# First operations of a unit tied behind traced evacuations, VectorE triangles and spread weight fetches in a hybrid attention layer

## The chip, the cores and the metric

The kernel runs on one core of a Trainium2 chip. The metric is device time in microseconds (us) of one execution, the median over the runs shown; lower is better. TensorE is called PE in the views (PEld its weight loads), VectorE is DVE, ScalarE is ACT, GpSimd is POOL and SyncE, which issues most transfers, is SP.

## The reference

One post-norm residual layer over 1024 tokens of width 1024. The mixing width is split into eight forgetting-attention heads (FoX: softmax with a decay from a forget gate) and eight stick-breaking heads, each 64 wide, all with a SiLU gate and one output projection.

```python
def reference(x, c, w_ada, b_ada, w_in, b_f, w_out, ln_g, ln_b):
    ...
    u = (_layer_norm(x) * (1.0 + scale[:, None, :]) + shift[:, None, :]).astype(dtype)
    fq, fk, fv, fg, ff, sq, sk, sv, sg = _split_columns(u @ w_in[layer])
    f_cum = jnp.cumsum(jax.nn.log_sigmoid(ff + b_f[layer]), axis=1).transpose(0, 2, 1)
    ...
        # FoX, per query block
        s = einsum(q, k) * scale + (f_q[..., :, None] - f_k[..., None, :])
        y = einsum(softmax(where(causal, s, -inf)), v)
        # stick-breaking, per query block
        z = einsum(q, k) * scale
        log_keep = where(strict, log_sigmoid(-z), 0.0)
        later = cumsum(log_keep, axis=3, reverse=True) - log_keep
        y = einsum(where(strict, exp(log_sigmoid(z) + later), 0.0), v)
    ...
    y = concatenate([y_fox * silu(fg), y_sb * silu(sg)], axis=-1) @ w_out[layer]
    resid = ALPHA * x + gate[:, None, :] * y
    x = _layer_norm(resid, ln_g[layer], ln_b[layer]).astype(dtype)
```

## The kernel before

**Units.** The sixteen heads are eight pairs p, 0 to 3 stick-breaking and 4 to 7 FoX. A unit (p, h, i) is one block of 128 query rows of one head h of a pair. There are sixteen units to a pair, so 128, and unit 112, called `LAST` in the code, opens pair 7. That pair takes its units by two query blocks, from the longest rows down: (h 0; i 7, 6), (h 1; 7, 6), (h 0; 5, 4) and so on.

**A unit's path.** `att_scores` (L487) issues the score matmuls `S` (L501, L502) into one of two PSUM buffers. For FoX a row operation on VectorE (L508) adds the decay and the mask, which lie in `fb`, to `S`, and writes `a` and the row's extreme `nm`; ScalarE takes the exponential (L514); two small VectorE operations invert the row sum `l` (L515, L516). Then ScalarE and VectorE split the result into two fp16 halves (L480, L481, called a half below; `f` is their room), and SP issues a transposing transfer (L485) into `pt`. For stick-breaking ScalarE takes two sigmoids (L527, L528), VectorE one or two scans (L533, L537), GpSimd a product (L541), and the halves follow (L477, L478). Four units after its scores, `att_pv` issues the `pv` matmuls (L585); ScalarE and VectorE evacuate them to `ty` (L611, L612), GpSimd multiplies by the gate (L614), SP stores.

**Projections beside it.** Between the units TensorE runs projections of the next pair as fillers, each a group of `m` matmuls (L284 to L286) or `v` matmuls (L355 to L357) into one of two accumulators. They are evacuated by a ScalarE and a VectorE operation: q (L255, L256), k (L264, L268 or L272, which write the low part `kl`), the gate (L277, L278, `sg`), v (L366, L367), and the small ones around the scale of v (`bss_sb`, L391 to L397) and the forget rows (`fcum`, L426 to L436).

**Triangles.** `att_causal` (L460) adds the causal triangle to a 128x128 block of `fb` (L465) ahead of each unit's row operation; it is issued behind the row operation of the unit before.

**Output projection.** `load_wo` (L924) fetches a 128-row slab `wor` of the output weights on SP's queue (L936, 512 KB), casts it in two pieces on ScalarE (`woh`, L939) and takes the rest on GpSimd (`wol`, L940). Two slabs are fetched at the first unit of pair 7; the others follow inside `gen_last_g`, the last projection (the gate of pair 7), two steps ahead. `load_ln` fetches the last layer norm's vectors (`lngb`). `o_half` runs the residual of half a block of rows: `gate` times the PSUM accumulator `o` into `r` (L1010), `ALPHA` times `xr` plus `r` (L1011), statistics (L1012). The accumulators `o` and `m` are the same two PSUM buffers.

**Rooms.** Six tiles of tag `att` hold `a`, `f`, `fb`, `kp`, `be` and `r`. Three wider tiles of tag `v` hold the v operands, the raw data of the first four slabs `wor` (two to a tile), `lngb`, the first two blocks' `xr` (`xr_two`), and, in some FoX pairs, two blocks' halves (`room_ff`).

**What sets the order.** TensorE's order is written out by hand by the loop at the end (`FILL`, `G7`, `TAIL` share the fillers out to units). The order on VectorE, ScalarE, GpSimd and SP is made by a scheduler at build time, from the program's dependences. `after(...)` adds an edge for that order only: on the chip each engine runs its own list in order and waits by semaphores for data and rooms alone.

## Time and profile before

| | |
|---|---|
| Median of 3 runs | 666.49 us |
| Lowest, highest | 664.18, 672.92 us |
| The profiled execution | 668.8 us |
| Its span | 667.0 us |
| Mean granted TensorE clock of its span | 0.979 |

The span is the time from the first to the last recorded instruction; the rest of the execution's time, 1.8 us, lies around it. The rows that the prediction rests on are shown there. A row of the timeline has its start, its duration, the engine, the line, the operation with its output and inputs, and, in brackets, how long the engine had been idle before it and what released it. Rows of consecutive equal operations are merged (x6). Tile names are without numbers there; in the order lists below a name has the head, the block and a running number, as `a_0_7_6048` for `a` of head 0, block 7.

### The profile page before, as it was taken

How to read it: one execution, taken by the hardware profiler on the slowest of the kernel's cores; microseconds unless marked ns; L12 is line 12 of the kernel's file. 1: busy time of each engine (PE TensorE's matmuls, PEld its weight loads, DVE VectorE, ACT ScalarE, POOL GpSimd, SP SyncE). 2: the span in 40 equal slices, each digit the busy share in tenths (PEclk: the TensorE clock that was granted, in tenths of full speed). 3: DMA queues.
4: the chain of work that ended last, by engine and by line, in shares of the span. 5: the costliest groups of instructions: out<-in, count | busy, mean ns of one | idle time of the engine just before them, and what ended most of it. 6: DMA issues, size and time to landing. Idle time of an engine off the chain costs nothing.

```text
span 667.0 us, 10848 instructions
## 1 busy us (share of the span) xinstructions
PE 620.2 (93%) x3523; PEld 524.4 (79%) x3523; DVE 494.1 (74%) x878; ACT 403.3 (60%) x803; POOL 413.4 (62%) x529
## 2 busy tenths in 40 slices
PE   5999999999999799998989999999999957799995
PEld 3779898888897678888978888899887736588885
DVE  6785458886869788897678777766888566896856
ACT  5567457876658667776666675766778775430000
POOL 6469978565649675877387454525643599656411
PEclk9999999999999899998999999999999977899998
DMA  9966331114635656556556766755566999552411
GB/s 332 410 254 250 95 96 40 30 29 113 127 75 104 150 90 148 122 134 144 106 145 149 170 145 139 177 134 131 143 139 150 248 240 226 141 156 102 154 64 63
DMA packets 169576, 97.79 MB, mean 147 GB/s; under 512 B 136944, under 2 KB 150576, under 8 KB 169520
## 3 DMA queue, kind: packets, MB, share of 16 engines
q1 hardware_dynamic: 158960, 76.61, 45.6%
q10 hardware_dynamic: 10560, 20.50, 11.3%
q8 instruction: 28, 0.46, 0.3%
q14 instruction: 28, 0.23, 0.1%
HBM read 51.95 MB, written 7.90 MB: 90 GB/s over the span
## 4 chain that ended last, share of the span: by engine, by line
PE 67%; DVE 8%; DMA 7%; issue 6%; ACT 5%; POOL 5%; SPq 1%; ACTq 0%; POOLq 0%; DVEq 0%
PE m L284 8%; PE m L285 7%; PE m L286 7%; PE pv L585 6%; PE o L991 4%; PE o L993 4%; PE o L992 4%; PE S L501 4%; PE S L502 4%; PE v L355 3%; PE v L357 3%; PE v L356 3%; POOL be L541 2%; DMA raws<-in_w_qkg_dram 2%; DMA pt<-kp 2%
## 5 line engine op out<-in xcount | busy, mean ns | idle before, releaser
L284 PE MATMUL m<-uh,whi 128*128 128x512 f32 x304 | 124.3, 409 | 4.5 <-DVE bss_sb L394 2.3
L286 PE MATMUL m<-uh,wlo 128*128 128x512 f32 x304 | 120.4, 396 | 0.0
L285 PE MATMUL m<-ul,whi 128*128 128x512 f32 x304 | 120.3, 396 | 0.0
L541 POOL TENSOR_TENSOR be<-be,kp 128x127 f32<-128x127 f32 (+3 forms) x64 | 86.4, 1351 | 35.5 <-DVE kp L537 19.0
L481 DVE SCALAR_TENSOR_TENSOR f<-a,l,f 128x1024 f16<-128x1024 f32 (+3 forms) x64 | 70.6, 1109 | 24.0 <-ACT f L480 23.3
L614 POOL TENSOR_TENSOR ty<-ty,sg 64x256 f32<-64x256 f32 x64 | 53.4, 835 | 48.8 <-DVE ty L612 30.3
L501 PE MATMUL S<-k,q 128*128 128x512 f32 (+5 forms) x192 | 67.7, 354 | 11.7 <-DVE nm L508 11.7
L533 DVE TENSOR_TENSOR_SCAN kp<-kp,floor 128x512 f32<-128x512 f32 (+2 forms) x64 | 65.1, 1017 | 15.6 <-ACT kp L527 14.6
L284 PEld LDWEIGHTS m<-uh,whi 128*128 128x128 f32 x304 | 57.6, 190 | 15.1 <-DVE bss_sb L394 2.7
L286 PEld LDWEIGHTS m<-uh,wlo 128*128 128x128 f32 x304 | 57.5, 189 | 13.7
L465 POOL TENSOR_TENSOR fb<-fb,causal 128x128 f32<-128x128 f32 x64 | 37.8, 592 | 49.1 <-DVE nm L508 35.6
L514 ACT ACTIVATE a<-a,nm 128x1024 f32<-128x1024 f32 (+3 forms) x64 | 49.6, 774 | 28.9 <-DVE nm L508 27.8
L585 PE MATMUL pv<-pt,v 128*128 128x256 f16 (+1 forms) x560 | 65.3, 264 | 1.3 <-DVE ty L612 0.7
L502 PE MATMUL S<-kl,qz 128*128 128x512 f32 (+5 forms) x192 | 66.3, 346 | 0.0
L285 PEld LDWEIGHTS m<-ul,whi 128*128 128x128 f32 x304 | 57.6, 189 | 9.3
L585 PEld LDWEIGHTS <-v 128*128 128x128 f16 x560 | 48.2, 98 | 17.8 <-issue 10.1
L480 ACT ACTIVATE f<-a,l 128x1024 f16<-128x1024 f32 (+3 forms) x64 | 49.1, 773 | 20.8 <-DVE l L516 13.6
L478 DVE TENSOR_TENSOR kp<-be,kp 128x128 f16<-128x128 f32 (+7 forms) x48 | 50.0, 1042 | 15.0 <-ACT kp L477 14.6
L355 PE MATMUL v<-whi_v,uh 128*128 128x256 f32 (+1 forms) x192 | 56.1, 292 | 3.6 <-DVE kl L268 2.5
L508 DVE CUSTOM_DVE_ANT_0 a<-S,fb 128x1024 f32<-128x1024 f32 (+3 forms) x64 | 48.2, 753 | 10.7 <-POOL fb L465 4.2
L527 ACT ACTIVATE kp<-S 128x128 f32<-128x128 f32 (+3 forms) x64 | 41.6, 651 | 22.8 <-PE S L502 14.9
L357 PE MATMUL v<-wlo_v,uh 128*128 128x256 f32 (+1 forms) x192 | 54.8, 285 | 0.0
(314 smaller groups left out, 1603.2 us busy)
## 6 DMA issues: line engine op xcount, KB each, us to landing
raw<-in_w_qkg_dram ACTq DMA_DIRECT2D x38, 256.0 KB, 2.7
wss<-in_w_ss_dram SPq DMA_DIRECT2D x16, 512.0 KB, 8.4
wg<-in_w_gate_dram SPq DMA_DIRECT2D x8, 512.0 KB, 4.1
fb<-f_dr ACTq DMA_DIRECT2D x8, 512.0 KB, 4.4
wor<-in_w_out_dram SPq DMA_DIRECT2D x8, 512.0 KB, 6.1
out_dram<-r SPq DMA_DIRECT2D x15, 256.0 KB, 2.0
y_dr<-ty SPq DMA_DIRECT2D x56, 64.0 KB, 2.0
x<-in_x_dram SPq DMA_DIRECT2D x6, 512.0 KB, 5.6
```

The costliest lines, as they stand in the source:

```text
L284: nc.tensor.matmul(acc, hi[:, c], u_hi[kt][:, s], start=(kt == 0), stop=False)
L285: nc.tensor.matmul(acc, hi[:, c], u_lo[kt][:, s], start=False, stop=False)
L286: nc.tensor.matmul(acc, lo[:, c], u_hi[kt][:, s], start=False, stop=(kt == NB - 1))
L355: nc.tensor.matmul(acc[:, :n], u_hi[kt][:, ts_], hi[:, s], start=(kt == 0), stop=False)
L357: nc.tensor.matmul(acc[:, :n], u_hi[kt][:, ts_], lo[:, s], start=False, stop=(kt == NB - 1))
L481: nc.vector.scalar_tensor_tensor(second, a3, l, first, op0=ALU.mult, op1=ALU.subtract)
L501: nc.tensor.matmul(S[:, s, :w], qst[p][h][:, qs], kst[p][h][:, ks], start=True, stop=False)
L502: nc.tensor.matmul(S[:, s, :w], z, klo[p][:, ks], start=False, stop=True)
L533: scan = nc.vector.tensor_tensor_scan(rv, rv, floor[0][:, 512 - n:][:, ::-1], initial=0.0, op0=ALU.mult, op1=ALU.max)
L541: nc.gpsimd.tensor_tensor(be[:, :ke - 1], be[:, :ke - 1], kp[:, 1:ke], op=ALU.mult)
L585: nc.tensor.matmul(acc[:, q0:256], vt[p][:, kb, h * P:h * P + P], st_pt[p, h, j][:, 2 * kb + part, q0:], start=start, stop=stop)
L614: nc.gpsimd.tensor_tensor(yt[r, :], yt[r, :], sgt[p][r, qs], op=ALU.mult)
```

## The change

Four things are changed.

1. `ev_ops` remembers the last evacuation's ScalarE and VectorE operation. The next unit's `att_scores` takes them and puts its own first ScalarE operation (the sigmoid, or the exponential) and its first VectorE operation (the scan, or the row operation) behind them, by edges of order alone.
2. The sixteen triangles of pair 7 run on VectorE instead of GpSimd.
3. The output weights' slabs are fetched at the units 111, 113, 114, 115, 117, 118, 119 and 120 instead of two at 112 and the others with the last projection; `load_ln` goes from unit 117 to 119; the halves of pair 6 that use a `v` tile are now blocks 7 to 4 of head 1 and all of head 0, instead of all of head 1 and blocks 5 to 0 of head 0.
4. In `o_half` the product with `gate` is written back into PSUM, and the second operation reads it there and writes `r`.

```diff
+    ev_ops = {}
     def evac_q(p, ch, acc, qst, heads):
...
-            nc.scalar.activation(qst[h][r, s], acc[r, :], AF.Copy, scale=SCALE)
-            nc.vector.scalar_tensor_tensor(qst[h][o, s], acc[r, :], SCALE, qst[h].bitcast(F32)[r, s],
-                                           op0=ALU.mult, op1=ALU.subtract)
+            ev_ops["act"] = nc.scalar.activation(qst[h][r, s], acc[r, :], AF.Copy, scale=SCALE)
+            ev_ops["dve"] = nc.vector.scalar_tensor_tensor(qst[h][o, s], acc[r, :], SCALE, qst[h].bitcast(F32)[r, s],
+                                                          op0=ALU.mult, op1=ALU.subtract)
...
     def evac_k(p, ch, acc, kst, klo, heads):
...
+        ev_ops.update(act=first, dve=last)
         return first, last
...
-        nc.vector.tensor_scalar(power, total, 1.0e-30, 1.0, op0=ALU.max, op1=ALU.mult)
+        ev_ops["dve"] = nc.vector.tensor_scalar(power, total, 1.0e-30, 1.0, op0=ALU.max, op1=ALU.mult)
...
     def att_causal(u):
...
-            nc.gpsimd.tensor_tensor(f[:, dg], f[:, dg], causal, op=ALU.add)
+            (nc.vector if p == 7 else nc.gpsimd).tensor_tensor(f[:, dg], f[:, dg], causal, op=ALU.add)
...
     def att_scores(u, following):
...
+        behind = [ev_ops.pop(e) for e in list(ev_ops)]
...
-            rows = nc.vector.tensor_tensor_reduce(out=v3(a), in0=S[:, :ns, :w], in1=v3(f),
+            with after(*behind):
+                rows = nc.vector.tensor_tensor_reduce(out=v3(a), in0=S[:, :ns, :w], in1=v3(f),
...
-            nc.scalar.activation(a[:, :ke], a[:, :ke], AF.Exp, scale=-1.0, bias=nm, accum_out=l)
+            with after(*behind):
+                nc.scalar.activation(a[:, :ke], a[:, :ke], AF.Exp, scale=-1.0, bias=nm, accum_out=l)
...
-            if p == 4 or (p == 5 and h == 0) or (p == 6 and (h or i < 6)):
+            if p == 4 or (p == 5 and h == 0) or (p == 6 and (h == 0 and i < 6 or i > 3)):
...
-            nc.scalar.activation(v3(kp), S[:, :ns, :w], AF.Sigmoid, scale=-1.0)
+            with after(*behind):
+                nc.scalar.activation(v3(kp), S[:, :ns, :w], AF.Sigmoid, scale=-1.0)
...
-            scan = nc.vector.tensor_tensor_scan(rv, rv, floor[0][:, 512 - n:][:, ::-1], initial=0.0,
-                                                op0=ALU.mult, op1=ALU.max)
+            with after(*behind):
+                scan = nc.vector.tensor_tensor_scan(rv, rv, floor[0][:, 512 - n:][:, ::-1], initial=0.0,
+                                                    op0=ALU.mult, op1=ALU.max)
...
     def o_half(t, h):
...
-        nc.vector.tensor_tensor(r[:, s], o_acc[t, h][:, :s.stop - s.start], gate[:, s], op=ALU.mult)
-        nc.vector.scalar_tensor_tensor(r[:, s], xr[:, s], ALPHA, r[:, s], op0=ALU.mult, op1=ALU.add)
+        oa = o_acc[t, h][:, :s.stop - s.start]
+        nc.vector.tensor_tensor(oa, oa, gate[:, s], op=ALU.mult)
+        nc.vector.scalar_tensor_tensor(r[:, s], xr[:, s], ALPHA, oa, op0=ALU.mult, op1=ALU.add)
...
     def gen_last_g(p):
...
-            if kt + 2 < NB:
-                load_wo(kt + 2)
...
+    WOLOAD = [16 * (NPAIR - 1) + d for d in (-1, 1, 2, 3, 5, 6, 7, 8)]
...
-        if k == LAST:
-            for pr in range(2):
-                load_wo(pr)
+        if k in WOLOAD:
+            load_wo(WOLOAD.index(k))
...
-        if k == LAST + 5:
+        if k == LAST + 7:
             load_ln()
```

The other evacuations (gate, v, forget rows, `ty`) are recorded in the same way. TensorE's own list is the same in both kernels. The lists of the other engines differ; three places follow, each before and then after. Lines of the changed kernel have other numbers (L508 is L514 there, L939 is L948, L940 is L949, L465 is L469, L1010 and L1011 are L1020 and L1021).

ScalarE at the start of pair 7, before (`qz` are the queries' casts, `a_0_7` the pair's first unit, `ty_1_2` an evacuation of pair 6):

```order
L480 ACTIVATE f_1_0_5944<-a_1_1_5936,l_1_1_5938 128x2x128
L480 ACTIVATE f_1_0_5944<-a_1_0_5987,l_1_0_5989 128x128
L458 CAST qz_83<-q_0_5569 64x128
L611 ACTIVATE ty_1_2_6075<-pv_1_2_6062,bss_sb 64x256
L514 ACTIVATE a_0_7_6048,l_0_7_6050<-a_0_7_6048,nm_0_7_6049 128x1024
L480 ACTIVATE f_0_7_6056<-a_0_7_6048,l_0_7_6050 128x8x128
L458 CAST qz_84<-q_0_5569 64x128
L514 ACTIVATE a_0_6_6114,l_0_6_6116<-a_0_6_6114,nm_0_6_6115 128x896
L939 CAST woh_6010<-wor_6012 128x512 x2
L458 CAST qz_85<-q_1_5570 64x128
L939 CAST woh_6024<-wor_6012 128x512 x2
```

and after:

```order
L521 ACTIVATE a_1_1_5936,l_1_1_5938<-a_1_1_5936,nm_1_1_5937 128x256
L462 CAST qz_83<-q_0_5568 64x128
L620 ACTIVATE ty_1_2_6069<-pv_1_2_6056,bss_sb 64x256
L484 ACTIVATE f_1_1_5944<-a_1_1_5936,l_1_1_5938 128x2x128
L521 ACTIVATE a_1_0_5987,l_1_0_5989<-a_1_0_5987,nm_1_0_5988 128x128
L948 CAST woh_6156<-wor_6158 128x512 x2
L462 CAST qz_84<-q_0_5568 64x128
L484 ACTIVATE f_1_0_5995<-a_1_0_5987,l_1_0_5989 128x128
L448 DMA fb_6000<-f_dr 128x1024
L948 CAST woh_6188<-wor_6158 128x512 x2
L521 ACTIVATE a_0_7_6042,l_0_7_6044<-a_0_7_6042,nm_0_7_6043 128x1024
L462 CAST qz_85<-q_1_5569 64x128
```

The casts of four slabs, eight operations, and `ty_1_2` now stand ahead of the first unit's exponential, and the load of the last `fb` stands behind the last half of pair 6; before, the first casts stood behind the second unit's exponential.

GpSimd in the first half of pair 7, before (`wol` the splits of the output weights, `fb` the triangles, `whi_y` and `wlo_y` splits of stored outputs):

```order
L465 TENSOR_TENSOR fb_5999<-fb_5999,causal 128x128
L972 TENSOR_TENSOR wlo_y_0_6347<-yr_0_6344,whi_y_0_6346 128x512
L614 TENSOR_TENSOR ty_1_0_6260<-ty_1_0_6260,sg_5368 64x256
L940 TENSOR_TENSOR wol_6087<-wor_6088,woh_6086 128x512 x2
L465 TENSOR_TENSOR fb_5679<-fb_5679,causal 128x128
L940 TENSOR_TENSOR wol_6134<-wor_6135,woh_6133 128x512 x2
L940 TENSOR_TENSOR wol_6167<-wor_6168,woh_6166 128x512 x2
L940 TENSOR_TENSOR wol_6195<-wor_6196,woh_6194 128x512 x2
L614 TENSOR_TENSOR ty_0_3_6330<-ty_0_3_6330,sg_6001 64x256
L465 TENSOR_TENSOR fb_5679<-fb_5679,causal 128x128
L465 TENSOR_TENSOR fb_5999<-fb_5999,causal 128x128
```

and after, from the same product `ty_1_0` on:

```order
L623 TENSOR_TENSOR ty_1_0_6229<-ty_1_0_6229,sg_5368 64x256
L949 TENSOR_TENSOR wol_6261<-wor_6262,woh_6260 128x512 x2
L949 TENSOR_TENSOR wol_6319<-wor_6320,woh_6318 128x512 x2
L980 TENSOR_SCALAR whi_y_4_6334<-yr_4_6332 128x384
L981 TENSOR_TENSOR wlo_y_4_6335<-yr_4_6332,whi_y_4_6334 128x384
L623 TENSOR_TENSOR ty_0_3_6304<-ty_0_3_6304,sg_6002 64x256
L949 TENSOR_TENSOR wol_6363<-wor_6364,woh_6362 128x512 x2
L629 TENSOR_TENSOR y7l<-ty_0_3_6304,y7h 64x256
```

No triangle stands between the splits any more, and of sixteen splits the first eight now stand ahead of `ty_1_1`.

VectorE at the first residual of the output (`o_0` and `o_1` the two accumulators), before:

```order
L508 ISA a_1_2_6505,nm_1_2_6506<-S_1_2_6502,fb_5999 128x384
L508 ISA nm_1_2_6506 128x1
L481 SCALAR_TENSOR_TENSOR f_1_3_6471<-a_1_3_6463,l_1_3_6465,f_1_3_6471 128x4x128
L515 RECIPROCAL l_1_2_6507<-l_1_2_6507 128x1
L516 TENSOR_SCALAR l_1_2_6507<-l_1_2_6507 128x1
L1010 TENSOR_TENSOR r_6529<-o_0_6283,gate 128x512
L1010 TENSOR_TENSOR r_6529<-o_1_6287,gate 128x512
L612 SCALAR_TENSOR_TENSOR ty_1_2_6581<-pv_1_2_6568,bss_sb,ty_1_2_6581 64x256
L481 SCALAR_TENSOR_TENSOR f_1_2_6513<-a_1_2_6505,l_1_2_6507,f_1_2_6513 128x3x128
L1011 SCALAR_TENSOR_TENSOR r_6529<-xr_two,r_6529 128x512 x2
```

and after:

```order
L1020 TENSOR_TENSOR o_0_6252<-o_0_6252,gate 128x512
L523 TENSOR_SCALAR l_1_3_6466<-l_1_3_6466 128x1
L1020 TENSOR_TENSOR o_1_6256<-o_1_6256,gate 128x512
L514 ISA a_1_2_6506,nm_1_2_6507<-S_1_2_6503,fb_6000 128x384
L514 ISA nm_1_2_6507 128x1
L469 TENSOR_TENSOR fb_5678<-fb_5678,causal 128x128
L485 SCALAR_TENSOR_TENSOR f_1_3_6472<-a_1_3_6464,l_1_3_6466,f_1_3_6472 128x4x128
L522 RECIPROCAL l_1_2_6508<-l_1_2_6508 128x1
L523 TENSOR_SCALAR l_1_2_6508<-l_1_2_6508 128x1
L621 SCALAR_TENSOR_TENSOR ty_1_2_6582<-pv_1_2_6569,bss_sb,ty_1_2_6582 64x256
L1021 SCALAR_TENSOR_TENSOR r_6530<-xr_two,o_0_6252 128x512
L1021 SCALAR_TENSOR_TENSOR r_6530<-xr_two,o_1_6256 128x512
```

The two products stand ahead of the row operation of `a_1_2` and the half `f_1_3` now; the operation that reads them again stands behind both, with a triangle, the small operations and `ty_1_2` between.

More of the change, by code (lines that the diff above doesn't have):

```diff
@@ L276, in evac_g @@
         s = slice(ch * 512, ch * 512 + 512)
-        nc.scalar.activation(sg[:, s], acc, AF.Tanh, scale=0.5)
-        nc.vector.scalar_tensor_tensor(sg[:, s], sg[:, s], 1.0, acc, op0=ALU.add, op1=ALU.mult)
+        ev_ops["act"] = nc.scalar.activation(sg[:, s], acc, AF.Tanh, scale=0.5)
+        ev_ops["dve"] = nc.vector.scalar_tensor_tensor(sg[:, s], sg[:, s], 1.0, acc, op0=ALU.add, op1=ALU.mult)
     def m_step(acc, tiles, kt, ch):
@@ L368, in v_tile @@
                                           apply_absolute_value=True)]
+        ev_ops.update(act=v_last[0], dve=v_last[1])
         if g == 1:
-            nc.vector.tensor_tensor(fsb[:, :, t], acc[:, 256:264], bf_sb, op=ALU.add)
+            ev_ops["dve"] = nc.vector.tensor_tensor(fsb[:, :, t], acc[:, 256:264], bf_sb, op=ALU.add)
         yield
@@ L431, in forget_rows @@
         fc = cp.tile([P, 64], F32, tag="fab", name="fc")
-        nc.vector.scalar_tensor_tensor(fc, fp[:, :64], -1.0, pre, op0=ALU.mult, op1=ALU.subtract)
+        ev_ops["dve"] = nc.vector.scalar_tensor_tensor(fc, fp[:, :64], -1.0, pre, op0=ALU.mult, op1=ALU.subtract)
         yield
@@ L435, in forget_rows @@
         nc.tensor.transpose(ft, fc, ident)
-        nc.scalar.copy(fr, ft)
+        ev_ops["act"] = nc.scalar.copy(fr, ft)
         nc.sync.dma_start(f_dr.rearrange("h (t p) -> (h t) p", p=P), fr)
@@ L507, in att_scores @@
             l = sb.tile([P, 1], F32, tag="l", bufs=4, name=f"l_{p}_{h}_{i}")
-            rows = nc.vector.tensor_tensor_reduce(out=v3(a), in0=S[:, :ns, :w], in1=v3(f),
-                                           op0=ALU.add, op1=ALU.min, scale=-1.0, scalar=BIG,
-                                           accum_out=nm)
+            with after(*behind):
+                rows = nc.vector.tensor_tensor_reduce(out=v3(a), in0=S[:, :ns, :w], in1=v3(f),
+                                                      op0=ALU.add, op1=ALU.min, scale=-1.0, scalar=BIG,
+                                                      accum_out=nm)
             if following:
@@ L610, in att_pv @@
         tm, yt = ty[:, :256], ty[:, 256:]
-        nc.scalar.activation(tm[r, :], acc[o, :256], AF.Copy, scale=1.0 / CW if down is None else down[o, :])
-        nc.vector.scalar_tensor_tensor(yt[r, :], acc[r, :256], 1.0 / CW if down is None else down[r, :], tm[r, :],
+        ev_ops["act"] = nc.scalar.activation(tm[r, :], acc[o, :256], AF.Copy, scale=1.0 / CW if down is None else down[o, :])
+        ev_ops["dve"] = nc.vector.scalar_tensor_tensor(yt[r, :], acc[r, :256], 1.0 / CW if down is None else down[r, :], tm[r, :],
                                        op0=ALU.mult, op1=ALU.add)
```

## The prediction

> **What bounds the kernel now.** I read the page's shares first, then its chain, then the waits of TensorE, and then each stretch in which TensorE waits, row by row.
>
> ```profile
> span 667.0 us, 10848 instructions
> PE 620.2 (93%) x3523; PEld 524.4 (79%) x3523; DVE 494.1 (74%) x878; ACT 403.3 (60%) x803; POOL 413.4 (62%) x529
> PE 67%; DVE 8%; DMA 7%; issue 6%; ACT 5%; POOL 5%; SPq 1%; ACTq 0%; POOLq 0%; DVEq 0%
> ...
> PE S L501 <- DVE nm L508: 11.7, 4, 4.1
> ...
> PE o L991 <- DVE r L1010: 2.9, 1, 2.9
> PE v L355 <- DVE kl L268: 2.5, 1, 2.5
> PE m L284 <- DVE bss_sb L394: 2.3, 1, 2.3
> PE o L991 <- DVE sg L278: 1.9, 1, 1.9
> ...
> PE m L284 <- DVE q L256: 1.2, 1, 1.2
> ...
> PE m L284 <- DVE kl L272: 1.1, 1, 1.1
> ```
>
> TensorE is busy for 93% and carries 67% of the chain. So only its waits can be won (waits: total us, times, longest). Four of them end with an evacuation on VectorE (2.5, 2.3, 1.2, 1.1); those are what the ties aim at. 11.7 + 2.9 + 1.9 lie in the last head pair. Its stretches (columns: stretch; busy and count of PE, PEld, DVE, ACT, POOL; clock; DMA share; GB/s):
>
> ```profile
> 520.00:540.00 20.00, 15.11 (x77) 12.19 (x76) 12.08 (x22) 16.72 (x31) 15.28 (x15) 0.93 0.97 245
> 540.00:560.00 20.00, 13.93 (x65) 10.58 (x63) 11.72 (x21) 11.95 (x22) 19.84 (x18) 0.82 1.09 268
> 560.00:580.00 20.00, 14.50 (x65) 11.45 (x66) 15.76 (x31) 10.08 (x23) 14.20 (x21) 0.87 0.66 133
> ```
>
> In 540–560 GpSimd is full (19.84 of 20), VectorE is not (11.72), and the granted clock falls to 0.82. Its rows and VectorE's and TensorE's there:
>
> ```profile
> 549.34 0.45 POOL L465 TENSOR_TENSOR fb<-fb,causal 128x128 f32<-128x128 f32 x1
> 549.76 8.06 POOL L940 TENSOR_TENSOR wol<-wor,woh 128x512 fp32r<-128x512 f32 x6
> ...
> 549.83 0.82 DVE L508 CUSTOM_DVE_ANT_0 a<-S,fb 128x640 f32<-128x640 f32 x1 [2.40 <-POOL fb L465]
> ...
> 560.06 0.82 DVE L508 CUSTOM_DVE_ANT_0 a<-S,fb 128x640 f32<-128x640 f32 x1 [0.91 <-POOL fb L465]
> ...
> 550.81 0.60 PE L501 MATMUL S<-k,q 128*128 128x320 f32 x1 [4.12 <-DVE nm L508]
> ...
> 552.01 0.63 PE L991 MATMUL o<-woh,whi_y 128*128 128x512 f32 x1
> 552.44 0.63 PE L992 MATMUL o<-woh,wlo_y 128*128 128x512 f32 x1
> ...
> 556.73 0.39 PE L992 MATMUL o<-woh,wlo_y 128*128 128x512 f32 x1
> 556.97 0.39 PE L993 MATMUL o<-wol,whi_y 128*128 128x512 f32 x1
> ...
> 561.04 0.66 PE L501 MATMUL S<-k,q 128*128 128x384 f32 x1 [2.99 <-DVE nm L508]
> ```
>
> A triangle of 0.45 us stands behind splits of the output weights on GpSimd, the row operation waits for the triangle, and TensorE for the row operation: 4.12, then 2.99. Behind the wait, matmuls start 0.43 us apart (552.01, 552.44) instead of 0.24 (556.73, 556.97). The first wait of the pair has another cause:
>
> ```profile
> 525.46 9.56 DMA pt<-f
> ...
> 535.18 1.09 DVE L508 CUSTOM_DVE_ANT_0 a<-S,fb 128x896 f32<-128x896 f32 x1 [2.66 <-DMA pt<-f]
> ...
> 536.34 0.41 PE L501 MATMUL S<-k,q 128*128 128x320 f32 x1 [2.98 <-DVE nm L508]
> ```
>
> A transpose issued behind four 512 KB loads takes 9.56 us to land (the first row, from the chain), and its source's room is what the row operation waits for: 2.98 on TensorE. With 4.12 and 2.99 that leaves 1.6 of the 11.7 for a fourth wait of this kind.
>
> **The ties.** They move operations and add none.
>
> ```profile
> 345.56 2.03 DVE L481 SCALAR_TENSOR_TENSOR f<-a,l,f 128x1024 f16<-128x1024 f32 x1 [1.28 <-ACT f L480]
> ...
> 306.40 0.40 DVE L533 TENSOR_TENSOR_SCAN kp<-kp,floor 128x128 f32<-128x128 f32 x1
> ...
> 307.47 0.69 DVE L268 TENSOR_TENSOR kl<-m,k 64x512 fp32r<-64x512 f32 x1
> ```
>
> At 347 the 2.03 us half now stands behind L394: −2.0. At 307 the second `kl` passes a scan and a `ty`, 307.47 − 306.40 = 1.1 between the starts: −0.9 of 2.5, as its own cast must be done too. At 516 the casts of k and their `kl` pass a row operation and a half: −1.0 of 1.1. At 247 q passes the scans and a half, but ScalarE's next in-order work then waits for it: −0.6 of 1.2. Sum −4.5. What is late next are the passed scans and halves, and behind them GpSimd's products, the transposes and pv four units on. That is at most two `kl` and one half, 2 × 0.69 + 2.03 = 3.4, and I take +1.0, since pv follows its scores by four units and most of such a delay ends in that distance. Net **−3.5** (ends −7.1, all four waits, and +3.4). The wait of 3.1 for `fcum` stays: nothing moves there.
>
> **Start of the last pair: loads spread, casts and DMA order.** Loads of `wor` now come from one unit ahead of the pair on, so the four no longer stand together ahead of the first transpose; but lngb and `xr_two` now do on SyncE, and these need rooms that GpSimd's splits of the first four `wor` free. On ScalarE eight casts now stand ahead of the first exps.
>
> ```profile
> L939 ACT CAST woh<-wor x16: 603/615/623, 525.2 to 549.3; 128x512 fp32r<-128x512 f32 x16
> ...
> L940 POOL TENSOR_TENSOR wol<-wor,woh x16: 1261/1283/2153, 525.9 to 556.5; 128x512 fp32r<-128x512 f32 x16
> ...
> fb<-f_dr ACTq DMA_DIRECT2D x8, 512.0 KB, 4.4
> ```
>
> Eight casts are 8 × 0.615 = 4.9 us. Idle time of ScalarE hides a part that the order doesn't tell, so the first four units come later by up to 4.9; the waits of 2.98 and 1.90 that end at 536 and 539, 4.9 together, go in exchange, since they waited for the same units. I take **0** (ends −4.9 and +4.9). The last `fb` is issued behind two exps, two halves and three groups of casts more than before on ScalarE and takes 4.4 us to land; its first triangle now stands on VectorE ahead of the first unit's half, so VectorE would wait there with all that is behind it. The third unit is the first to need this `fb`, and a wait is within the +4.9.
>
> **Triangles.** 16 leave GpSimd and go to VectorE, where a 128x128 operation is bounded by this row from below, and by GpSimd's own 0.45 from above:
>
> ```profile
> 516.04 0.29 DVE L508 CUSTOM_DVE_ANT_0 a<-S,fb 128x128 f32<-128x128 f32 x1
> ...
> 516.33 0.60 DVE L481 SCALAR_TENSOR_TENSOR f<-a,l,f 128x384 f16<-128x384 f32 x1
> ...
> 571.09 3.04 DVE L481 SCALAR_TENSOR_TENSOR f<-a,l,f 128x384 f16<-128x384 f32 x1 [0.30 <-ACT f L480]
> ```
>
> 4.12 + 2.99 = 7.1 of TensorE's waits go; five triangles stand ahead of row operations in that stretch, 5 × 0.29 = 1.4. **−5.7**. Ends: −8.7 if the fourth wait of 1.6 goes as well and the triangles cost nothing, −2.7 if only VectorE's own waits go (2.40 + 0.91 − 2 × 0.29). I take the value near the upper end, because without triangles no row operation of the pair waits for GpSimd.
>
> The last two rows are one operation of one shape: 0.60 us and 3.04 us, the latter beside work of GpSimd. [...]
>
> **Clock.** The slow rows behind 4.12 and 2.99 are five matmuls each, 0.43 − 0.24 = 0.19 more: 2 × 5 × 0.19 = 1.9; the wait that ends at 536 has as many again behind it, an estimate of 1.6. I take **−1.3**, two thirds of 1.9, as the waits may shrink without vanishing (ends 0 and −3.5).
>
> **Gate product in place.** No instruction more; but PSUM is held until L1011 has read it, and in the new order eight or nine rows stand between the two.
>
> ```profile
> 576.18 1.28 DVE L1010 TENSOR_TENSOR r<-o,gate 128x512 f32<-128x512 f32 x2
> ...
> 578.55 1.82 DVE L1011 SCALAR_TENSOR_TENSOR r<-xr_two,r 128x512 f32<-128x512 f32 x2
> ```
>
> TensorE waited 2.9 for the first of these products. Now it waits for the first L1011. At the least that adds L1011 itself, 0.9; if both stay where they are, it adds 578.55 + 0.91 − 576.18 − 0.64 = 2.6. The new order puts the products ahead of a row operation and a half, and these between the products and L1011, which moves one end towards the other; I take the middle, **+1.7** (ends 0, should the wait be covered, and +2.6). Later halves: 24 matmuls × 0.24 = 5.8 us on the other buffer cover 1.28 + 0.91, so 0; without that cover it would be 15 × 0.9 = 14.
>
> **Rooms.** Halves of pair 6 change between the two kinds of room, one tile fewer of the scarcer kind: 0, ends ±2.8, all that row operations wait for transposes:
>
> ```profile
>   DMA pt<-f: 2.8, 2
> ```
>
> **Sum.** −3.5 + 0 − 5.7 − 1.3 + 1.7 + 0 = −8.8. The profiled execution took 668.8 us, 1.8 more than its span; 668.8 − 8.8 = 660.0. The median of the runs, 666.49, is 2.3 below that execution: 657.7.
>
> **Rivals.** B, nothing is given back: ties −4.5, triangles −8.7, clock −3.5, the rest 0 is −16.7, so 649.8 by the median. For it speaks that VectorE is busy for only 39.6 of the 60 us of 520–580 by the windows; against it the lockstep of in-order ScalarE, whose casts come earlier. C, moved triangles wait for GpSimd's splits all the same: six beside splits × 1.28 = 7.7 and the 1.3 of clock gone, −8.8 + 9.0 = +0.2, so 666.7. For it the 3.04 row, against it that the row operation, which reads `S` in PSUM and `fb`, ran in 0.82 beside the six splits at 549.8. E, the ties do nothing, since each wait goes to the next evacuation: −5.3, so 661.2; the moved order at 347 speaks against it. D, the other side: SyncE is stuck at `xr_two` until eight splits are done. If they take 2.15 each, 17.2 us, and delay the transpose of 525.46 by as much, the later waits vanish into it (−7.1), ties −3.5 and in-place +1.7 stay: +8.3, so 674.8. It decides from a delay of 9 us on, that is an issue after 534. Against it: the splits now start earlier, ahead of the stretch in which GpSimd is full.
>
> **Chances.** Forecast (654 to 663) 0.45, B (644 to 653) 0.27, C 0.14, E 0.08, D 0.06. The range 648 to 668 leaves out half of B and the most of D, near 0.2. A measurement of this kernel tells about 2% from no change, 653.2 and 679.8 us: below lies B, 0.27; above, a third of D, 0.02, should the later waits stay beside it (674.8 + 7.1 = 681.9); between, 0.71.
>
> **What would show it.** Right: waits of TensorE at 247, 307, 347 and 516 under half; no row operation behind GpSimd in the last pair; clock above 0.9 in 540–560; the wait ahead of `o` near 577 ended by the second operation of the residual. Wrong: triangle rows on VectorE over 1 us (C), the first transpose of the pair issued later than before by over 9 us (D), new waits of TensorE in pairs 5 and 6 (rooms, given-back halves), or waits gone from 540–560 with no gain, which would mean the casts at the pair's start cost their full 4.9.

## The result and the profile after

| | before | after |
|---|---|---|
| Median of 14 runs each, us | 667.48 | 676.01 |
| Lowest, highest, us | 664.18, 672.92 | 672.94, 677.56 |
| Ratio, 95% interval | | 1.0119 [1.0097, 1.0141] |
| Span of the profiled execution, us | 667.0 | 675.3 |
| Mean granted clock of the span | 0.979 | 0.974 |

The change makes the kernel slower by 667.48 × 0.0119 = 7.9 us (6.5 to 9.4). The forecast was 657.7, with a range up to 668.

The median of the three runs shown at first, 666.49, lies 1.0 below that of all 14. From the page of the changed kernel:

```profile
span 675.3 us, 10838 instructions
PE 623.8 (92%) x3523; PEld 525.4 (78%) x3523; DVE 499.2 (74%) x894; ACT 402.6 (60%) x803; POOL 404.1 (60%) x513
```

From its view of waits (engine, operation, line, and what ended the wait: total us, times, longest):

```profile
PE S L506 <- DVE nm L514: 13.3, 6, 4.4
PE v L358 <- DVE kl L270: 5.2, 1, 5.2
...
PE pv L594 <- DMA pt<-f: 2.8, 1, 2.8
PE o L1000 <- DVE r L1021: 2.5, 1, 2.5
...
PE S L506 <- issue: 1.2, 1, 1.2
...
PE m L287 <- DVE kl L274: 0.7, 1, 0.7
...
PE o L1000 <- DVE sg L281: 0.7, 1, 0.7
```

TensorE's waits for `bss_sb` (2.3) and for q (1.2) are gone, but that for a `kl` grew from 2.5 to 5.2, those for row operations went from 11.7 in four places to 13.3 in six, and 2.8 behind a transpose and 1.2 behind nothing that the profile names are new. The last head pair by stretches, columns as in the prediction:

```profile
520.00:540.00 20.00, 15.04 (x72) 11.08 (x70) 12.69 (x29) 14.03 (x31) 13.93 (x13) 0.91 1.01 223
540.00:560.00 20.00, 14.97 (x71) 12.08 (x70) 15.58 (x29) 13.87 (x25) 11.92 (x11) 0.83 0.98 238
560.00:580.00 20.00, 12.94 (x60) 9.21 (x59) 16.25 (x31) 11.34 (x26) 15.23 (x15) 0.83 0.75 185
```

GpSimd is no longer full in 540–560 (11.92 us instead of 19.84), as forecast. But most of that is not the triangles' move: of the splits of the output weights, four (5.98 us) lie in this stretch now instead of eleven (14.05), and of VectorE's increase from 11.72 to 15.58 four triangles make 2.75. TensorE waits as before (4.38 at 549.91, 4.12 at 550.81 before) and the clock is 0.83.

Where the time was lost can be read from one row per unit: the start of its first score matmul in the timeline, after minus before. I call this difference the lag.

| unit | before | after | lag | what lies ahead of it |
|---|---|---|---|---|
| (2,1,0) | 241.73 | 240.99 | −0.74 | |
| (2,1,4) | 256.15 | 254.67 | −1.48 | the wait for q at 247 is gone |
| (3,1,0) | 301.53 | 300.97 | −0.56 | |
| (3,1,4) | 320.49 | 324.24 | +3.75 | the wait for `kl`, 5.2 |
| (4,0,3) | 357.31 | 358.57 | +1.26 | the wait for `bss_sb` at 347 is gone |
| (5,0,7) | 402.22 | 406.27 | +4.05 | new waits at 373 and 396 |
| (5,1,3) | 452.10 | 457.93 | +5.83 | a new wait at 450, for an evacuation of v |
| (7,0,7) | 518.31 | 524.16 | +5.85 | the last pair starts |
| (7,1,6) | 528.55 | 540.73 | +12.18 | the wait for a transpose, 2.8 |
| (7,0,4) | 536.34 | 549.91 | +13.57 | |
| (7,1,4) | 550.81 | 558.81 | +8.00 | before's wait of 4.12 is gone |
| (7,1,2) | 569.20 | 579.57 | +10.37 | a wait of 4.0 behind a triangle |
| (7,1,0) | 588.15 | 596.48 | +8.33 | |

So the lag was 5.85 when the last pair began. 5.82 of it stood at the start of pair 6, up to which only the ties act on the order, but 0.89 stood already at the very first unit (90.36 against 89.47). 6.3 more came at the pair's start; of that 3.85 came back (12.18 − 8.33). Single traces differ by some us from chance (−1.6 to +1.3 at one wait, in the last section), so the verdicts below go by medians of many runs, and lags only say where.

### The profile page after: what moved, and what is told of

Read it like the earlier page. It is cut to its first block, busy times and chain, and to the rows that moved or that the text cites. A ratio compares the mean times of both kernels' runs of the same rounds, so it can differ in the third digit from the quotient of the medians.

```text
span 675.3 us, 10838 instructions
## 1 busy us (share of the span) xinstructions
PE 623.8 (92%) x3523; PEld 525.4 (78%) x3523; DVE 499.2 (74%) x894; ACT 402.6 (60%) x803; POOL 404.1 (60%) x513
## 3 DMA queue, kind: packets, MB, share of 16 engines
q10 hardware_dynamic: 10560, 20.50, 11.7%
## 5 line engine op out<-in xcount | busy, mean ns | idle before, releaser
L550 POOL TENSOR_TENSOR be<-be,kp 128x127 f32<-128x127 f32 (+3 forms) x64 | 84.0, 1315 | 41.8 <-DVE kp L546 21.3
L506 PE MATMUL S<-k,q 128*128 128x512 f32 (+5 forms) x192 | 68.3, 357 | 15.5 <-DVE nm L514 13.3
L485 DVE SCALAR_TENSOR_TENSOR f<-a,l,f 128x1024 f16<-128x1024 f32 (+3 forms) x64 | 64.5, 1009 | 17.0 <-ACT f L484 16.0
L594 PE MATMUL pv<-pt,v 128*128 128x256 f16 (+1 forms) x560 | 67.2, 269 | 4.9 <-DMA pt<-f 2.8
L482 DVE TENSOR_TENSOR kp<-be,kp 128x128 f16<-128x128 f32 (+7 forms) x48 | 52.8, 1103 | 14.4 <-ACT kp L481 13.9
L506 PEld LDWEIGHTS S<-k,q 128*128 128x128 f32 x192 | 36.9, 192 | 24.8 <-DVE nm L514 10.1
L359 PE MATMUL v<-whi_v,ul 128*128 128x256 f32 (+1 forms) x192 | 55.1, 287 | 0.0
L514 DVE CUSTOM_DVE_ANT_0 a<-S,fb 128x1024 f32<-128x1024 f32 (+3 forms) x64 | 48.2, 753 | 9.1 <-DMA pt<-f 5.4
```

The costliest lines, as they stand in the source:

```text
L359: nc.tensor.matmul(acc[:, :n], u_lo[kt][:, ts_], hi[:, s], start=False, stop=False)
L485: nc.vector.scalar_tensor_tensor(second, a3, l, first, op0=ALU.mult, op1=ALU.subtract)
L506: nc.tensor.matmul(S[:, s, :w], qst[p][h][:, qs], kst[p][h][:, ks], start=True, stop=False)
L550: nc.gpsimd.tensor_tensor(be[:, :ke - 1], be[:, :ke - 1], kp[:, 1:ke], op=ALU.mult)
L594: nc.tensor.matmul(acc[:, q0:256], vt[p][:, kb, h * P:h * P + P], st_pt[p, h, j][:, 2 * kb + part, q0:], start=start, stop=stop)
```

## The experiments

Each kernel was timed beside the kernel before, with 8 to 12 runs, but only 4 for the old gate product and for the triangles on GpSimd in the whole change. Differences are in us against the kernel before, from the ratio, with its 95% interval.

| kernel | median | difference |
|---|---|---|
| ties alone | 670.04 | +3.1 [0.9, 5.3] |
| triangles alone | 664.57 | −2.4 [−4.5, −0.3] |
| fetches and rooms alone | 671.16 | +4.1 [1.6, 6.6] |
| gate product alone | 670.62 | +3.3 [1.3, 5.3] |
| ties without those of `evac_k` | 669.03 | +1.6 [−0.1, 3.3] |
| ties, two units left out | 669.41 | +2.0 [0.2, 3.7] |
| triangles, ties without `evac_k` | 666.27 | −1.2 [−3.2, 0.7] |
| rooms alone | 669.45 | +3.5 [1.1, 5.9] |
| fetches alone, old rooms | 664.75 | −2.0 [−4.4, 0.4] |
| rooms, fetches tied behind transposes | 668.04 | +0.9 [−1.2, 3.0] |
| whole change without ties | 670.76 | +2.3 [0.2, 4.5] |
| whole change, old rooms | 672.55 | +5.6 [3.6, 7.6] |
| whole change, old gate product | 675.26 | +7.0 [4.5, 9.5] |
| whole change, triangles on GpSimd | 674.79 | +6.6 [4.7, 8.5] |
| triangles, fetches, old rooms, ties without `evac_k` | 668.39 | +0.4 [−1.7, 2.5] |
| triangles and fetches, old rooms | 664.15 | −2.4 [−4.1, −0.8] |

**The four parts, each alone.** The edits against the kernel before are the change's own lines, one group each:

```diff
# ties alone
+        behind = [ev_ops.pop(e) for e in list(ev_ops)]
+            with after(*behind):
# triangles alone
+            (nc.vector if p == 7 else nc.gpsimd).tensor_tensor(f[:, dg], f[:, dg], causal, op=ALU.add)
# fetches and rooms alone
+        if k in WOLOAD:
+            load_wo(WOLOAD.index(k))
+        if k == LAST + 7:
+            if p == 4 or (p == 5 and h == 0) or (p == 6 and (h == 0 and i < 6 or i > 3)):
# gate product alone
+        nc.vector.tensor_tensor(oa, oa, gate[:, s], op=ALU.mult)
+        nc.vector.scalar_tensor_tensor(r[:, s], xr[:, s], ALPHA, oa, op0=ALU.mult, op1=ALU.add)
```

> Only the ties are added to the kernel before; loads, rooms, triangles and the gate product stay as they were. Theory T (the ties themselves lose): in the changed kernel the score matmuls' lag grew by 5 us between the second and the seventh pair, so 667.5 + 4 to 6 = 671.5 to 673.5, with the wait at 347 gone and a wait of about 5 us near 310. Rival R (the ties are neutral and the lag came from elsewhere): 665 to 669. Rival P (the prediction's term was right and something else took it back): 663 to 665.

> Only the triangles of pair 7 go to VectorE. Theory T: the waits behind GpSimd near 550 and 561 (4.1 and 3.0) go and part comes back, 662 to 665. Rival C (the triangle waits on VectorE for GpSimd's splits all the same, rows over 1 us): 666 to 670.

> Only the fetches of the output weights, the layer norm's vectors and the rooms of pair 6 are changed. Theory T (the slabs, issued ahead of pair 6's last transposes, hold these and with them pv, ScalarE's in-order evacuation and the last pair's first units): 667.5 + 5 to 8 = 672.5 to 675.5, with a wait of TensorE for a transpose near 520. Rival R (in the changed kernel the ties' order made that collision): 666 to 670.

> Only the gate product is written back into PSUM. Theory T: one wait for an accumulator grows by up to 2.6, 667 to 670. Rival R (later halves have no cover): 672 to 680. Rival N (the second operation has one SBUF input less and is shorter beside GpSimd): 664 to 667.

Measured: +3.1, −2.4, +4.1, +3.3. The triangles (664.57) fell where expected; the ties (670.04) fell between two ranges, the fetches and rooms (671.16) below theirs, and the gate product (670.62) just above its own. The four add up to +8.1, and the whole change costs +7.9; with intervals of about 2 us to each side of each part, so close a fit is partly luck. So no part alone explains the loss; three of four cost, and the fourth gains less than forecast. For the gate product the timeline of its kernel shows the price in three rows:

```profile
577.52 0.69 DVE L1020 TENSOR_TENSOR o<-o,gate 128x512 f32<-128x512 f32 x1
...
581.45 1.28 DVE L1021 SCALAR_TENSOR_TENSOR r<-xr_two,o 128x512 f32<-128x512 f32 x2
...
582.19 0.50 PE L1000 MATMUL o<-woh,whi_y 128*128 128x512 f32 x1 [4.68 <-DVE r L1021]
```

The product is done at 578.2, but the accumulator is free only behind L1021, whose first half ends at 581.45 + 0.64 = 582.09; TensorE goes on there, after 4.68 idle. The lag of this trace grows there by 1.9, from +3.47 at unit (7,0,1) to +5.32 at (7,0,0). The +3.47 ahead of it arose in parts of the program that this kernel shares with the kernel before, so it is chance (this execution, 674.12, was the slowest of its ten).

**What the ties cost, and where.** The wait at 311 in the changed kernel, from its timeline:

```profile
306.18 1.99 POOL L550 TENSOR_TENSOR be<-be,kp 128x1023 f32<-128x1023 f32 x1
306.36 3.98 DVE L482 TENSOR_TENSOR kp<-be,kp 128x896 f16<-128x896 f32 x1
308.13 1.25 POOL L138 TENSOR_TENSOR wlo<-raw,whi 128x512 fp32r<-128x512 f32 x1
310.37 0.69 DVE L270 TENSOR_TENSOR kl<-m,k 64x512 fp32r<-64x512 f32 x1
311.21 0.55 PE L358 MATMUL v<-whi_v,uh 128*128 128x256 f32 x1 [5.16 <-DVE kl L270]
```

The same half and product in the timeline of the kernel before:

```profile
304.81 1.07 DVE L478 TENSOR_TENSOR kp<-be,kp 128x896 f16<-128x896 f32 x1
304.98 2.75 POOL L541 TENSOR_TENSOR be<-be,kp 128x1023 f32<-128x1023 f32 x1 [0.57 <-DVE kp L537]
```

Before, the half began 0.17 us ahead of GpSimd's product and took 1.07. Tied, it begins 0.18 us behind it and takes 3.98, until about 1.0 us after the split that GpSimd runs next has ended (308.13 + 1.25 = 309.38). TensorE waits for the `kl` behind it. At 247 q came earlier by the ties as well: the lag falls by 1.42 at (2,1,2), from −0.74 to −2.16. But it is back at −1.05 three units later and at −0.56 at (3,1,0). To test whether leaving the guilty ties out cures it, two kernels were made from the one with the ties alone:

```diff
# without those of evac_k
-        ev_ops.update(act=first, dve=last)
# two units left out
+        if u in ((3, 1, 0), (4, 1, 4)):
+            behind = []
```

> The ties as in the change, but without those of the evacuations of k; all else as before. Theory T (the ties of k lose, since they pull the second kl behind a half that GpSimd's operations hold for 4 us; the others gain at 247 and 347): the wait near 310 is back at about 2.5, those at 247 and 347 stay away, 667.4 - 2.5 to - 3.5 = 664 to 665. Rival R (any tie loses, through ScalarE's waits in order): 668 to 671.

> The ties alone, without those of the units (3, 1, 0) and (4, 1, 4). Theory T (a tied row operation reads its scores late and with two score buffers holds the unit after next): the wait of 1.4 near 396 goes, the one of 5 near 310 stays, since the second kl stands behind the half whether the scan is tied or not; 670.0 - 1.7 = 667 to 669. Rival (these waits have other causes): 670 to 671, both waits stay.

Measured: 669.03 and 669.41, which is the first one's rival and above the second one's 667 to 669: +1.6 and +2.0, against +3.1 for all ties; the three intervals overlap. Without the ties of `evac_k` the half and the wait at 310 are as before the change. From that kernel's timeline:

```profile
307.19 1.07 DVE L481 TENSOR_TENSOR kp<-be,kp 128x896 f16<-128x896 f32 x1
...
310.42 0.55 PE L357 MATMUL v<-whi_v,uh 128*128 128x256 f32 x1 [2.94 <-DVE kl L270]
```

The same holds in every trace of this document: in the six kernels with the ties of `evac_k` this half takes 3.98 to 4.06, in the twelve others 1.06 or 1.07. Leaving out the two units removed the wait at 396, as expected, but another came. Its timeline:

```profile
306.60 4.06 DVE L482 TENSOR_TENSOR kp<-be,kp 128x896 f16<-128x896 f32 x1
...
311.53 0.55 PE L358 MATMUL v<-whi_v,uh 128*128 128x256 f32 x1 [5.56 <-DVE kl L270]
...
426.87 0.45 PE L508 MATMUL S<-k,q 128*128 128x384 f32 x1 [1.17 <-DVE nm L516]
```

The wait at 396 is gone from this kernel, but the half at 306 is held for 4.06, as in the changed kernel, and 1.17 is new at 427. I had aimed at one tie, and the order there is evidently set by other units' ties as well. What such a new wait is made of shows best in the kernel without the ties of `evac_k`, in its timeline around unit (5,0,4), whose scores start at 417.66:

```profile
421.04 0.68 DVE L258 SCALAR_TENSOR_TENSOR q<-m,q 64x512 fp32r<-64x512 f32 x1
421.86 1.10 DVE L484 SCALAR_TENSOR_TENSOR f<-a,l,f 128x768 f16<-128x768 f32 x1
...
423.72 0.83 DVE L513 CUSTOM_DVE_ANT_0 a<-S,fb 128x640 f32<-128x640 f32 x1
424.61 0.44 PE L505 MATMUL S<-k,q 128*128 128x384 f32 x1 [1.20 <-DVE nm L513]
```

and in that of the kernel before, where those scores start at 417.81:

```profile
419.60 0.82 DVE L508 CUSTOM_DVE_ANT_0 a<-S,fb 128x640 f32<-128x640 f32 x1
```

The row operation is the tied one. It now stands behind the low parts of q and a half and starts 4.1 us later. It is also the operation that frees the score buffer, and there are two of those, so TensorE stands at the scores two units on, for 1.20. In the changed kernel it is the wait at 396:

```profile
396.73 0.45 PE L506 MATMUL S<-k,q 128*128 128x384 f32 x1 [1.44 <-DVE nm L514]
```

Between 370 and 480 each of the nine traced kernels with ties of any form has such a wait of 1.16 to 1.44, near 396 or 425, and none of the nine without ties has one.

Inside the whole change the ties were left out:

```diff
-        behind = [ev_ops.pop(e) for e in list(ev_ops)]
+        behind = []
```

> The whole change without its ties. If the parts add in the whole change: 676.0 - 3.1 = 671 to 674. Rival (in the whole change the ties' lag meets the early slabs, so more comes back): 668 to 671.

Measured: 670.76, which is the rival's range: 5.3 under the whole change, and the intervals of the two ratios do not meet. Inside the whole change no other part costs as much by the medians; alone, ties and rooms cannot be told apart. A milder form, ties without `evac_k` on top of the triangles, and the same with the spread fetches in the old rooms, gave:

> Triangles on VectorE and the ties without those of k; loads, rooms and the gate product as before. If the two gains add: 667.4 - 2.4 - 3 = 661 to 663. Rival R (a gain of the ties arrives at the last pair as a wait, whose start is set by other things): 664 to 666.

> Triangles, spread fetches with the old rooms, and the ties without those of k; gate product as before. If the ties without k are neutral to +2: 663 to 666. Rival P (they gain once the last pair has slack): 659 to 661.

Measured: 666.27, no gain over the triangles alone (664.57), and 668.39, where the same kernel without ties takes 664.15; both lie above every range expected. No form of the ties that ran gained anything.

**Rooms against fetches.** The third part holds two edits, which were taken apart: the new room rule alone, and the new fetches with the old rule.

```diff
# rooms alone
+            if p == 4 or (p == 5 and h == 0) or (p == 6 and (h == 0 and i < 6 or i > 3)):
# fetches alone, old rooms: WOLOAD and LAST + 7 as in the change, and
             if p == 4 or (p == 5 and h == 0) or (p == 6 and (h or i < 6)):
```

> Only the rule for the rooms of pair 6's halves is changed; the program asks for the slabs where the kernel before does. Theory T (the rule frees a wide tile earlier, and the scheduler sends the slabs ahead of pair 6's last transposes): 667.4 + 3 to 5 = 670.5 to 672.5, a wait of TensorE near 515 to 525. Rival R (the spread program points of the slabs are what costs): 666 to 668.5.

> The slabs and the layer norm's vectors are asked for as in the change, the rooms of pair 6 follow the old rule. Theory T (the rooms alone cost): 664 to 668, slabs issued behind pair 6's transposes as before. Rival R (the spread program points cost): 670.5 to 672.5.

Measured: 669.45, 1 below the range expected, so +3.5 [1.1, 5.9] for the room rule, and 664.75, so −2.0 [−4.4, 0.4] for the fetches. The fetches do no harm; the rule does. SP's rows at the end of pair 6 with the new rule alone, and a row operation behind them:

```profile
514.57 0.81 SPq L945 DMA_DIRECT2D wor<-in_w_out_dram  x2
516.58 4.71 SPq L489 DMA_TRANSPOSE pt<-f  x2
...
526.47 0.29 DVE L514 CUSTOM_DVE_ANT_0 a<-S,fb 128x128 f32<-128x128 f32 x1 [4.72 <-DMA pt<-f]
```

and with the old rule and the new fetches:

```profile
514.17 5.31 SPq L489 DMA_TRANSPOSE pt<-f  x3
519.72 0.45 SPq L631 DMA_DIRECT2D y_dr<-ty  x1
520.27 2.60 SPq L489 DMA_TRANSPOSE pt<-f  x2
522.97 0.52 SPq L945 DMA_DIRECT2D wor<-in_w_out_dram  x1
```

The rule frees a wide tile earlier. The slabs `wor` live in these tiles, so two loads of 512 KB now go out ahead of pair 6's last transposes instead of behind them, and a row operation waits 4.72 us for the room that a transpose empties. The changed kernel itself shows the same. From its chain, the wait for a transpose:

```profile
520.25 8.25 DMA pt<-f
```

and from its timeline:

```profile
518.21 1.03 SPq L945 DMA_DIRECT2D wor<-in_w_out_dram  x2
520.25 5.03 SPq L489 DMA_TRANSPOSE pt<-f  x2
...
528.54 2.50 PE L594 MATMUL pv<-pt,v 128*128 128x256 f16 x12 [2.79 <-DMA pt<-f]
```

The transpose behind two slabs takes 8.25 us to land, and `pv` waits 2.79 for it. This is the start of the +6.3 in the lags. The twelve `pv` matmuls behind the wait take 2.50 us (1.38 in the kernel before), and the evacuation `ty` of this `pv` comes late too, at 531.64 on VectorE. In VectorE's order the first row operation of the pair stands behind that `ty` and two halves now (before, it stood ahead of the `ty`). The scores of two units on start 0.1 us after it has ended, so the 1.20 that the view puts down to nothing is probably a wait for it:

```profile
534.81 1.23 DVE L514 CUSTOM_DVE_ANT_0 a<-S,fb 128x1024 f32<-128x1024 f32 x1
...
536.15 0.47 PE L506 MATMUL S<-k,q 128*128 128x512 f32 x1 [1.20 <-issue]
```

Across the traces the rule decides the lag at this place: from (6,1,2), ahead of the first fetch, to (7,1,6) it grows by 3.7 to 8.3 in the seven kernels with the new rule, and by at most 0.7 in the ten others. Whether the slabs' place in the queue is all of it was asked by tying them, under the new rule, behind the last transpose issued:

```diff
+        last_t[0] = nc.sync.dma_start_transpose(st_pt[p, h, j][:, :2 * nb, qo:qo + P], room.bitcast(F16)[:, :nb * 256])
...
+        with after(last_t[0]):
+            nc.sync.dma_start(full, w_out[pr * P:(pr + 1) * P, :])
```

> The new rooms of pair 6 alone, and every slab's fetch tied by order behind the last transpose issued so far. Theory T (the loss of the new rooms is the early slabs, which the tie takes away): 666 to 668, no wait of TensorE over 1.5 between 515 and 530. Rival R (the four halves that now need the scarcer rooms cost, slabs or not): 669 to 671.

Measured: +0.9 [−1.2, 3.0]. From (6,1,2) to (7,1,6) the lag grows by 3.7 (from −0.87 to +2.86), and by 7.1 with the rule alone (from +1.54 to +8.66). So in these two traces about half of the growth goes with the order in the queue. The rest stays: the wait for `kl` at 517, which was expected not to be there, is 2.72 here and 2.73 with the rule alone, against 1.06 before. By the medians (669.45 and 668.04) the intervals overlap, and how much of the cost is order and how much is four halves in the scarcer rooms stays open. With the old rule inside the whole change:

> The whole change, but with the old rule for the rooms of pair 6. Theory T (the parts add: ties +3.1, triangles -2.4, loads with the old rooms -2.3, gate product +3.3): 667.2 + 1.7, 667 to 671. Rival R (in the whole change the ties make the collision by themselves): 673 to 677.

Measured: 672.55, which misses the 667 to 671 expected: 3.5 below the whole change by the medians, with ratios whose intervals overlap. In its trace the lag stays at +4.47 from (7,0,7) to (7,1,6), so the +6.3 at the pair's start is gone with the rule. What is left is +5.6 [3.6, 7.6], while the other parts alone sum to 3.1 + 3.3 − 2.4 − 2.0 = +2.0. The 3.6 between may mean that the parts cost more together than apart (the ties are 5.3 when left out of the whole and 3.1 alone), but five intervals of about 2 us to each side do not show it.

**The gate product and the triangles inside the whole change.** Each was undone by itself:

```diff
# old gate product
+        nc.vector.tensor_tensor(r[:, s], o_acc[t, h][:, :s.stop - s.start], gate[:, s], op=ALU.mult)
+        nc.vector.scalar_tensor_tensor(r[:, s], xr[:, s], ALPHA, r[:, s], op0=ALU.mult, op1=ALU.add)
# triangles on GpSimd
+            nc.gpsimd.tensor_tensor(f[:, dg], f[:, dg], causal, op=ALU.add)
```

> The whole change with the gate product in r as before. If the parts add: 676.0 - 3.3 = 672 to 674. Rival (the wait for the accumulator is hidden by the other lag): 675 to 677.

> The whole change with the triangles of the last pair on GpSimd as before. If the triangles gain in the whole change as they do alone: 676.0 + 2.4 = 677 to 680. Rival (with the lag from slabs and rooms, GpSimd is no longer what row operations wait for): 674 to 677.

Measured: 675.26 and 674.79, in the rivals' ranges, beside 676.01 for the whole. Neither can be told from the whole change. The triangles, which gain 2.4 alone, show no gain in it. Two things are seen there: behind the late start of the pair row operations wait for transposes and halves, and the triangles on VectorE are themselves held. The timeline of the changed kernel:

```profile
538.99 1.28 DVE L485 SCALAR_TENSOR_TENSOR f<-a,l,f 128x1024 f16<-128x1024 f32 x1
...
540.42 7.65 SPq L489 DMA_TRANSPOSE pt<-f  x2
...
548.76 1.09 DVE L514 CUSTOM_DVE_ANT_0 a<-S,fb 128x896 f32<-128x896 f32 x1 [4.08 <-DMA pt<-f]
...
549.91 0.64 PE L506 MATMUL S<-k,q 128*128 128x320 f32 x1 [4.38 <-DVE nm L514]
...
564.72 2.71 POOL L949 TENSOR_TENSOR wol<-wor,woh 128x512 fp32r<-128x512 f32 x2 [1.87 <-ACT woh L948]
...
567.68 3.06 DVE L469 TENSOR_TENSOR fb<-fb,causal 128x128 f32<-128x128 f32 x1
568.07 2.51 POOL L949 TENSOR_TENSOR wol<-wor,woh 128x512 fp32r<-128x512 f32 x2
...
573.80 0.77 PE L506 MATMUL S<-k,q 128*128 128x512 f32 x1 [3.97 <-DVE nm L514]
```

At 548.76 a row operation waits 4.08 for a transpose and TensorE 4.38 for it. At 567.68 a triangle on VectorE takes 3.06 us beside the splits, and TensorE waits 3.97 at the scores behind it. In this trace five of the sixteen triangles take over 1 us, and all together take 12.1, where 16 × 0.29 = 4.6 was forecast. With the triangles alone one takes over 1 us, and half are at most 0.35; by line (ns: least, median, most):

```profile
L469 DVE TENSOR_TENSOR fb<-fb,causal x16: 269/353/2103, 513.5 to 580.7; 128x128 f32<-128x128 f32 x16
```

**A version that beats both.** Triangles and spread fetches, with the old rooms, the old gate product and no ties:

> The two parts that gained, alone: triangles on VectorE and the spread fetches with the old rooms; no ties, gate product as before. If they add: 667.2 - 2.4 - 2.3 = 661.5 to 664. Rival R (both take away the same waits near 550 and 561): 664 to 666.

Measured: 664.15, 0.9964 [0.9939, 0.9988] of the kernel before. It is the lowest median here, but by only 0.4 below that of the triangles alone (664.57), so the two gains do not add; the rival's range was 664 to 666. Its TensorE still waits in the pair:

```profile
540.00:560.00 20.00, 15.78 (x91) 12.10 (x90) 19.59 (x33) 14.56 (x30) 18.07 (x16) 0.96 0.90 215
```

In 540–560 VectorE is now busy for 19.59 of 20 us and GpSimd for 18.07, so both are near their limit there, while the clock (0.96) and TensorE's busy time (15.78) are above those before (0.82, 13.93).

## Why the prediction was wrong, point by point

- **What bounds the kernel: right in the main.** Of the 8.3 us by which the two spans differ, 3.6 are in TensorE's busy time (620.2 and 623.8) and the rest, the larger part, is in its waits. Not all of the places were named: the new waits at 373 and 396 lie in pair 4, and new waits had been looked for in pairs 5 and 6.
- **The ties, −3.5: wrong, and the failing step is the give-back.** At 347 the lag fell by 2.5 (forecast 2.0). At 247 it fell by 1.4 (forecast 0.6), but all but 0.3 was back three units later. Both falls are in each of the nine traces with ties and in none without; at 516 the wait went from 1.1 to 0.7 in the whole change and to 1.35 with the ties alone (forecast −1.0). So the moved operations did come earlier at 347 and 247. The step that failed is "+1.0, since pv follows its scores by four units and most of such a delay ends in that distance". The tied operation is the one that reads the scores, and only two score buffers stand behind it; its delay is back at TensorE two units on, at 396 (1.44) and, in the other kernels, at 424 (1.20) and 427 (1.17). (The new wait at 450 is another one: 1.04 for an evacuation of v; with the ties alone it is not there.) At 307 the forecast −0.9 became a wait of 5.16 instead of 2.53, since the half that was passed then started behind GpSimd's product and took 3.98 instead of 1.07. Together the ties cost 3.1 alone (by the ratio) and 5.3 in the whole change (by the medians).
- **The start of the last pair, 0: wrong in its sign.** The lag grew by 6.3, beyond the upper end of 4.9. The new fetches, which I had weighed, cost nothing alone (−2.0 [−4.4, 0.4]). The eight casts, the 4.9 of that sum, were not tested by themselves: in the kernel with the fetches alone the first of them stand behind the second exponential, as before.
- **Rooms, 0 (ends ±2.8): mis-sized, and this is where that start went.** +3.5 [1.1, 5.9] alone. I had counted tiles of each kind, but not asked which entry of SP's queue the freed tile lets forward.
- **Triangles, −5.7: the mechanism right, the size off.** In the trace of the triangles alone the lag goes from −2.77 at (7,0,7) to −8.11 at (7,1,0), so −5.3 in the pair, but that execution was the fastest of its ten; the medians give −2.4 [−4.5, −0.3]. In the whole change, nothing that can be told from zero. The reason given, that no row operation would wait for GpSimd any more, held for the operation and not for the triangle ahead of it (3.06 at 567.68). Rival C happened in part: in the whole change five triangles took 1.12 to 3.06 us, and the mean of the sixteen was 0.76, above the 0.45 taken as the upper bound. That is 7.5 us more of VectorE's time than forecast, but only some of it held TensorE.
- **The clock, −1.3: did not come.** 0.83 in 540–560 (0.82 before). A wait of 4.38 stayed there (4.12 before), and behind it the granted clock was 0.50 from 549.9 to 555 (before: 0.50 from 550.8 to 554).
- **The gate product, +1.7: the mechanism right.** The wait ahead of `o` is ended by L1021, as forecast. Alone it takes 4.68 there instead of 2.9, +1.8 (the rows of the experiment); the medians say +3.3 [1.3, 5.3] alone, which includes 1.8. In the whole change the wait is 2.47, and undoing the part there gave 0.75 us, inside the noise.
- **Rival D: its sign and size came, its cause at most in part.** It gave 674.8 and asked for a first transpose of the pair issued after 534, behind `xr_two` and the first eight splits. That transpose was issued at 540.42, and `xr_two` ahead of it at 538.49, right behind the eighth split (538.47), until 540.31. But the half that it carries was finished only at 538.99 + 1.28 = 540.27, so the units were as late as SyncE. Nearly all of the lag (12.10 at (7,1,7)) was there before, and the ties, which D counted as −3.5, cost. So its number came by luck.
- **The chances.** Each part was given a likely gain or 0, and give-backs of +1.0 and +1.7. Three parts with a cost of over 3 us each were not among the cases.

## What to carry to other kernels

An edge of order ahead of the operation that frees a two-deep buffer cost here a wait of 1.16 to 1.44 us, two users of the buffer later, so look at what each tie puts ahead of it, not only at what it puts behind. When a rule for rooms changes, list which transfers get their room earlier and what stands behind those in the same queue. Price each part of such a change both alone and left out of the whole: here the parts' sum fitted (8.1 against 7.9), while one part's gain of 2.4 could not be found in the whole, so a sum that fits does not show that the parts act alike in the whole.

## What was not expected of the hardware

**One late start, several instructions of waiting.** The two rows at 304.81 and 304.98 and those at 306.18 to 308.13 are the same pair of operations with the order of their starts exchanged by 0.35 us: the half takes 1.07 or 3.98, the product 2.75 or 1.99. In these rows the one that starts second takes the longer of its two times. They show one thing more: the held half did not end with GpSimd's product (306.18 + 1.99 = 308.17) but at 306.36 + 3.98 = 310.34, when the next split had ended too (309.38). The long half is seen in all six kernels with the ties of `evac_k` (3.98 to 4.06) and is gone without them (1.06 or 1.07). That it was held by both of GpSimd's instructions is read from the rows; no kernel moved the split alone.

**Equal waits, different clocks behind them.** In the timeline of the kernel before, behind a wait of 3.09 us for `fcum`, with a granted clock of 0.50 in 230–233:

```profile
230.25 0.63 PE L286 MATMUL m<-uh,wlo 128*128 128x512 f32 x1
```

and in the changed kernel, behind a wait of 3.06 at the same place, with a granted clock of 1.00 in 230–233:

```profile
230.91 0.40 PE L289 MATMUL m<-uh,wlo 128*128 128x512 f32 x1
```

Nothing ahead of this place explains it: with the triangles alone the rows are of the quick kind (0.40, behind a wait of 3.05), and with the gate product alone, which acts 340 us later, of the slow one (0.63, behind 3.06). What decides it is not shown by any run here. Over the other kernels' traces the lag against the kernel before changes by −1.6 to +1.3 us across this one wait. For reading traces it means that such a lag between two single executions is no evidence of a change.
